# Two transformer blocks on one core: transposes of values a unit later, moving weights at another start, sums for three norms in other places

## The chip, the cores and the metric

One core of a Trainium2 chip runs the program. The metric is the device time of one execution in microseconds (us), as the median of several plain runs. The profiled execution is a further one, whose time is given beside its span.

## The reference, cut to what matters

Two blocks run one after the other on 256 tokens of width 1024, in fp32. In the first block 16 meta tokens are set ahead of the sequence, so that its products have 272 columns where keys and values need the meta tokens. It has a SwiGLU part, a mixer with two kinds of attention, and a second SwiGLU part. The second block has a mixer of convolution and retention, a cross attention to 256 memory tokens, and a squared-ReLU part.

```python
def first_block(x, ...):
    h = concat(pad, meta_tokens, x)
    h = h + 0.5 * swiglu(rms_norm(h, ffn1_norm), ffn1_w_in, ffn1_w_out)
    h = h + token_mixer(rms_norm(h, mix_norm), ...)   # qa ka va fa | qb kb vb | ga gb
    h = h + 0.5 * swiglu(rms_norm(h, ffn2_norm), ffn2_w_in, ffn2_w_out)
    return h[:, BLOCK:]

def token_mixer(h, ...):
    qa, ka, va, fa, qb, kb, vb, ga, gb = split(h @ w_in)
    # qa, ka, qb, kb: rms norm over each head of 64
    log_f = log_sigmoid(fa + forget_bias)             # its running sum enters the scores of fox
    y = sigmoid(ga) * (fox(qa, ka, va, log_f) @ w_branch_fox) \
      + sigmoid(gb) * (swa(qb, kb, vb, sinks, bias) @ w_branch_swa)
    return y @ w_out

def second_block(x, mem, ...):
    mem_n = rmsnorm(mem, norm_mem_w)
    h = x + head_group_mixer(rmsnorm(x, norm_mix_w), ...)   # cg/cu gated conv, rq rk rv rg retention
    h = h + cross(rmsnorm(h, norm_xattn_w) @ xq_w, mem_n @ xkv_w) @ xo_w
    h = h + square(relu(rmsnorm(h, norm_mlp_w) @ up_w)) @ down_w
    return rmsnorm(h, norm_f_w)
```

## The kernel before

All weights stay in HBM and are streamed once through SBUF, in chunks of 2048 columns of fp32, by SP's DMA queue (`raw`). Each piece of up to 1024 columns is split into two parts that TensorE takes in its fp32r form: ScalarE copies it to the upper part `hi` (line 321), VectorE subtracts that from `raw` and gets the lower part `lo` (line 337). Activations are kept as an upper and a lower part too (`XH`, `XL`; `AHf`, `ALf`; `MH`, `ML` for the memory). Each product is three matmuls, `XH·hi`, `XL·hi` and `XH·lo` (`mm3`, lines 512 to 514). There the weights are the stationary operand, 128 x 128, and the activations move, 256 or 272 columns.

Only `products_t` (lines 1016 to 1028) is the other way round: a tile of activations is stationary and 512 columns of weights move. It makes the retention's values (`rv`, one call) and the memory's values (`xv`, two calls), with 8 `k` times 2 halves times 3 matmuls in each call, 144 in all.

`_part` (line 308) places the parts of a chunk in a tile that is 64 columns wider than the chunk, from a column that `shift` gives: `SHIFT` = 13 columns (52 bytes), or `SHIFT1` = 16 columns (64 bytes) for chunks that begin with a weight of `WITH_META`.

The order is written by hand. The program is a row of units, each made by `_Core.step` (line 401): the unit's matmuls `mm`, then a `hook`, then the evacuations of the unit before (`pending`), then background work `back`, then splits of weights ahead. Evacuations are generators: a plain `yield` lets one piece of weights be split, and `yield LATER` puts the rest off to the next unit's turn. So an evacuation's first part is issued after the next unit's matmuls, and what stands behind a `yield LATER` a unit after that. On each engine instructions run in this issued order.

PSUM has eight banks, five named `ps` and three `po`; `bank()` (line 449) hands them out in turn.

The places that the change touches:

- `value` (line 870): factors a value by the row factor `r` into `x` (line 872) and `rep` on VectorE, then has TensorE transpose both into a bank (lines 878 to 880), and a unit later copies it out: `vfm` (line 889) on VectorE, the rest on ScalarE. It serves the four units `va` and the unit `vb`. The projections run `ka`, `qa`, `fa`, `va`, `kb`, `qb`, `vb` and gates, and the attention's pairs of scores (line 669) begin between the unit `qb` 0 and the next.
- `key_s` and `key_like` (line 812): the sliding window's key, with squares (`sqh`), their sum per head by a matmul (line 778), a root, and the write to `ks`.
- `forget` (lines 790 to 810): a running sum over the tokens on VectorE, whose last step are two DMAs from POOL's queue (lines 809, 810) into rows of `kz`, which the scores read.
- `memory` (line 1002): background work during the second SwiGLU part, `f2` and `d2`: loads the memory, splits it into `MH` and `ML`, and adds its squares up in `accm`.
- `mixer2` (line 1031): the hook `stats` after the first unit of the convolution, `glu((0, 1))`, makes the row factor `r` of the mixer (line 561 and ScalarE's Ln and Exp, lines 555 and 556), and the memory's two factors `rm` and `rmc` (lines 1051 to 1055). The units' evacuations (`br`, `ar` line 1095, and so on) need `r`.

Of the kernel before, what the change touches and what calls it, by code (L numbers as in the profile page):

```python
# [10 lines left out]
F32 = mybir.dt.float32  # L11
# [15 lines left out]
SHIFT, SHIFT1 = 13, 16  # L27
WITH_META = ("f1g", "d1", "ka", "fa", "va")
DFF = 2816
MF = DFF // P  # L30
# [245 lines left out]
class _Weights:  # L276
# [3 lines left out]
    def __init__(self, nc, pool, ws):  # L280
        self.nc, self.pool, self.ws = nc, pool, ws
        chunks, self.where, self.start, self.ends, self.total = _plan()
        self.shift = [SHIFT1 if blocks[0][0][0] in WITH_META else SHIFT for blocks in chunks]
        self.raw, self.hi, self.lo = {}, {}, {}
        self.loaded = 0
        self.c, self.o = 0, 0
        self.begun = []
        self.done = 0
        self.used = 0
        self.free = 0  # L290
        self.beside = None
# [76 lines left out]
class _Core:  # L368
# [32 lines left out]
    def step(self, key, mm, evac=(), hook=None, bg=1, last=False, to=None,  # L401
             ahead=True, reach=1024):


        W = self.W
        end, to = W.span(key, to or key)
        W.split(end)
        mm()
        if hook:
            W.split(to)  # L410
            hook()
        work, self.pending = self.pending, []
        near = (min(to, W.done + reach) if last else to) if ahead else None
        self.run(work, near)
        self.pending = list(evac) + self.pending
        if last:
            W.split(near)
            self.drain()
        self.back(bg, to)
        if ahead:  # L420
            W.split(to)
# [8 lines left out]
def _program(ctx, tc, I, out, probe=None):  # L430
# [126 lines left out]

    def rms(acc, n):

        ps = bank()  # L560
        T.matmul(ps[:, :n], k0("ones"), acc, start=True, stop=True)
        r = tmp(base, "r")
        rsqrt(r[:, :n], ps[:, :n])
        return r
# [171 lines left out]
    def mixer(acc_in, acc_out):  # L736
        with tc.tile_pool(name="mixer", bufs=1, reuse_waits="tile") as pool:
# [73 lines left out]

            def key_like(ps, write):
                x = tmp(pool, "x", bufs=4)[:, :T1]
                V.tensor_tensor(x, ps[:, :T1], r[0][:, :T1], op=ALU.mult)
                yield
                root = head_norm(head_squares(x, T1), T1)
                yield LATER
                rc = root()
                yield
                for e in range(2):  # L820
                    write(e, slice(64 * e, 64 * e + 64), x, rc)
# [32 lines left out]
            def key_s(m, ps):  # L854
# [4 lines left out]

                return key_like(ps, write)  # L860

# [6 lines left out]
            def value(ps, dst, meta):  # L868
# [6 lines left out]
                                ps[:, SEQ:T1].unsqueeze(1).broadcast_to((P, H, NMETA)),  # L875
                                r[0][:, SEQ:T1].unsqueeze(1).broadcast_to((P, H, NMETA)), op=ALU.mult)
                vt = bank()
                T.transpose(vt[:, 0:P], x[:, :P], kc("id"))
# [122 lines left out]

    def memory(pool, MH, ML, accm):
        raw = pool.tile([P, KD, SEQ], F32, name="memraw")

        def one(k):
# [4 lines left out]
            add()  # L1010

        background.append(lambda: nc.sync.dma_start(raw, I["mt"]))
        background.extend([lambda: None] * 3)
        background.extend([lambda k=k: one(k) for k in range(KD)])

    def products_t(tag, j, x, evac, **kw):
# [14 lines left out]

    def mixer2(acc_in, acc_out, MH, ML, accm, kx, vx, rm, held):
        with tc.tile_pool(name="mixer2", bufs=1, reuse_waits="tile") as pool:
# [7 lines left out]
            cs = pool.tile([P, 2, SEQ], F32, name="cs")  # L1041
            rmc = pool.tile([P, 2], F32, name="rmc")
            nc.gpsimd.memset(U[:, :, :30], 0.0)
# [4 lines left out]
            def stats():  # L1048
                r.append(rms(acc_in[:, :SEQ], SEQ))
                ps, pc = bank(), bank()  # L1050
                T.matmul(ps[:, :SEQ], k0("ones"), accm, start=True, stop=True)
                for i in range(2):
                    T.matmul(pc[:, 2 * i : 2 * i + 2], accm[:, i * P : (i + 1) * P], k0("ones")[:, :2], start=True, stop=True)
                rsqrt(rm, ps[:, :SEQ])
                rsqrt(rmc, pc[:, 0:4:2])

# [20 lines left out]
            def glu(ms):  # L1077
                ab = {m: (bank(), bank()) for m in ms}

                def mm():  # L1080
                    cut = KD - 1 if len(ms) > 1 else KD
                    for part in (range(cut), range(cut, KD)):
                        for m in ms:
                            for k in part:
                                for o, t in zip(ab[m], "ug"):
                                    mm3(o[:, :SEQ], W.get(("c" + t, m, k)), xs(k), k == 0, k == KD - 1)

                def evac(m):
# [13 lines left out]
                step(("cg", ms[0], 0), mm, [lambda m=m: evac(m) for m in ms], hook=stats if ms[0] == 0 else None, bg=0,  # L1102
                     to=("cg", ms[-1], 0))

# [488 lines left out]
    accm = base.tile([P, SEQ], F32, name="accm")  # L1593
    rm = base.tile([P, SEQ], F32, name="rm")
    with tc.tile_pool(name="mem", bufs=1, side="right", reuse_waits="tile") as mpool:
        memory(mpool, MH, ML, accm)
        ffn("f2", "d2", SEQ, hB, "g_mix2", acc, acc2, bg=1, together=True)
# [5 lines left out]
    with tc.tile_pool(name="kvm", bufs=1, side="right", reuse_waits="tile") as kv:  # L1603
        kx = kv.tile([P, KD, SEQ], F32, name="kx")
        vx = kv.tile([P, 2, D], F32, name="vx")
        held = []
        mixer2(acc, acc2, MH, ML, accm, kx, vx, rm, held)
        probe("h4", hB)
# [21 lines left out]
```

## Time and profile before

| what | value |
|---|---|
| median of 3 plain runs | 954.95 us (954.78 to 955.3) |
| profiled execution | 955.88 us |
| its span in the trace | 954.1 us |
| mean granted clock of TensorE | 0.998 |
| busy: TensorE, VectorE, ScalarE, POOL | 99%, 71%, 56%, 1% of the span |
| read from HBM | 166.85 MB, 176 GB/s over the span |

The span runs from the first to the last recorded instruction; the execution's own time is 1.78 us longer. A matmul of 256 fp32r columns is recorded with some 280 ns although the next starts 113 to 120 ns later, because matmuls overlap in the array. For what one costs, the distance from one start to the next is read, not the duration. An idle time in brackets at the end of a row stands before that instruction, with the instruction that it waited for.

### The profile page before, as it was taken

To read this page: it belongs to the slowest core of one execution; us is meant where nothing else is said; L and a number is where in the kernel's file an instruction comes from. 1 tells how busy PE (TensorE), PEld (TensorE's weight loads), DVE (VectorE), ACT (ScalarE), POOL (GpSimd) and SP (SyncE) were. 2 spreads that over 40 slices of the span, in tenths; PEclk is the share of its full clock that TensorE was granted. 3 is DMA by queue.
4 is the path that set the end of the run, shared out by engine and by line. 5 is a ranking of instruction groups with operands and counts; after the bars stand their busy time and mean duration, and the time that the engine had idled before them with its cause. 6 is when DMAs were issued, how large, how long until landed. Compare 5 with 4: busy or idle time off the path is not lost.

```text
span 954.1 us, 18439 instructions
## 1 busy us (share of the span) xinstructions
PE 941.5 (99%) x7687; PEld 914.0 (96%) x7687; DVE 673.2 (71%) x1252; ACT 535.3 (56%) x930; POOL 10.2 (1%) x16
## 2 busy tenths in 40 slices
PE   9999999999999999999999999999999999999996
PEld 8999999999899999999999999888899999999996
DVE  6686556657886678678666667999976677775552
ACT  7555435446586566666544557546484566655441
POOL 0000000020000000000000000000000000000000
PEclk9999999999999999999999999999999999999999
DMA  9665527554333345655545565433543246655431
GB/s 327 197 253 177 177 91 243 175 181 176 133 133 130 107 144 193 238 198 208 180 176 179 196 244 212 162 133 140 217 164 143 89 177 221 211 196 212 177 133 45
DMA packets 30116, 169.12 MB, mean 177 GB/s; under 512 B 5048, under 2 KB 7488, under 8 KB 13392
## 3 DMA queue, kind: packets, MB, share of 16 engines
q1 hardware_dynamic: 29680, 167.41, 49.8%
q8 instruction: 60, 0.98, 0.4%
q10 hardware_dynamic: 288, 0.52, 0.1%
q14 instruction: 24, 0.20, 0.1%
q0 software_dynamic: 64, 0.01, 0.0%
HBM read 166.85 MB, written 1.07 MB: 176 GB/s over the span
## 4 chain that ended last, share of the span: by engine, by line
PE 71%; DVE 2%; ACT 2%; issue 0%; DVEq 0%; ACTq 0%
PE ps L512 14%; PE ps L513 14%; PE ps L514 14%; PE po L513 7%; PE po L512 7%; PE po L514 7%; PE ps L1028 1%; PE ps L1026 1%; PE ps L1027 1%; PE ps L669 1%; PE po L713 0%; DVE lo L337 0%; PE ps L1195 0%; DVE y L801 0%; PE po L1367 0%; PE ps L1329 0%
## 5 line engine op out<-in xcount | busy, mean ns | idle before, releaser
L337 DVE TENSOR_TENSOR lo<-raw,hi 128x1024 fp32r<-128x1024 f32 (+2 forms) x337 | 373.7, 1123 | 47.1 <-ACT hi L321 45.3
L321 ACT ACTIVATE hi<-raw 128x1024 fp32r<-128x1024 f32 (+2 forms) x337 | 322.0, 974 | 125.9 <-issue 44.1
L512 PE MATMUL ps<-XH,hi 128*128 128x256 f32 (+2 forms) x968 | 275.9, 285 | 0.5 <-ACT hi L321 0.5
L514 PE MATMUL ps<-XH,lo 128*128 128x256 f32 (+2 forms) x968 | 271.1, 280 | 0.0
L513 PE MATMUL ps<-XL,hi 128*128 128x256 f32 (+2 forms) x968 | 271.0, 280 | 0.0
L512 PEld LDWEIGHTS ps<-XH,hi 128*128 128x128 f32 (+1 forms) x968 | 181.1, 187 | 3.7 <-issue 1.3
L513 PEld LDWEIGHTS ps<-XL,hi 128*128 128x128 f32 (+1 forms) x968 | 181.5, 188 | 0.8
L514 PEld LDWEIGHTS ps<-XH,lo 128*128 128x128 f32 (+1 forms) x968 | 181.2, 187 | 0.5 <-DVE lo L337 0.2
L512 PE MATMUL po<-XH,hi 128*128 128x256 f32 (+1 forms) x464 | 131.6, 284 | 0.6 <-DVE ar L1095 0.6
L514 PE MATMUL po<-XH,lo 128*128 128x256 f32 (+1 forms) x464 | 130.1, 280 | 0.0
L513 PE MATMUL po<-XL,hi 128*128 128x256 f32 (+1 forms) x464 | 129.9, 280 | 0.0
L512 PEld LDWEIGHTS po<-XH,hi 128*128 128x128 f32 x464 | 87.4, 188 | 1.0 <-DVE ar L1095 0.8
L513 PEld LDWEIGHTS po<-XL,hi 128*128 128x128 f32 x464 | 87.2, 188 | 0.2
L514 PEld LDWEIGHTS po<-XH,lo 128*128 128x128 f32 x464 | 87.2, 188 | 0.0
L628 ACT ACTIVATE s<-gr 128x272 f32<-128x272 f32 (+1 forms) x44 | 18.7, 426 | 104.2 <-DVE gr L626 104.2
L512 PE MATMUL ps<-AHf,hi 128*128 128x272 f32 (+1 forms) x220 | 61.9, 281 | 0.0
L513 PE MATMUL ps<-ALf,hi 128*128 128x272 f32 (+1 forms) x220 | 61.9, 281 | 0.0
L514 PE MATMUL ps<-AHf,lo 128*128 128x272 f32 (+1 forms) x220 | 61.9, 281 | 0.0
L1066 DVE SCALAR_TENSOR_TENSOR cv<-U,par,cv 128x256 f32<-128x256 f32 x120 | 50.0, 475 | 0.2 <-ACT cv L1099 0.2
L514 PE MATMUL ps<-AHm,lo 128*128 128x256 f32 x160 | 44.2, 276 | 0.0
L512 PE MATMUL ps<-AHm,hi 128*128 128x256 f32 x160 | 44.2, 276 | 0.0
L513 PE MATMUL ps<-ALm,hi 128*128 128x256 f32 x160 | 44.2, 276 | 0.0
(391 smaller groups left out, 1780.2 us busy)
## 6 DMA issues: line engine op xcount, KB each, us to landing
raw<-in_ws_dram SPq DMA_DIRECT2D x128, 1024.0 KB, 4.9
raw<-in_ws_dram SPq DMA_DIRECT2D x32, 704.0 KB, 4.1
raw<-in_ws_dram SPq DMA_DIRECT2D x5, 512.0 KB, 6.7
dec<-in_dec_dram SPq DMA_DIRECT2D x1, 1536.0 KB, 7.4
hA<-in_xt_dram SPq DMA_DIRECT2D x2, 576.0 KB, 6.9
BM<-drow SPq DMA_DIRECT2D x2, 512.0 KB, 5.3
memraw<-in_mt_dram SPq DMA_DIRECT2D x1, 1024.0 KB, 7.0
cst<-in_cst_dram SPq DMA_DIRECT2D x1, 720.0 KB, 8.3
```

Source lines behind the costliest of these rows:

```text
L321: self.nc.scalar.activation(self.hi[c][:, a:b], self.raw[c][:, a:b], AF.Copy)
L337: self.nc.vector.tensor_tensor(self.lo[c][:, a:b], self.raw[c][:, a:b], self.hi[c][:, a:b].bitcast(F32), op=ALU.subtract)
L512: T.matmul(o, w[0], x[0], start=start, stop=False)
L513: T.matmul(o, w[0], x[1], start=False, stop=False)
L514: T.matmul(o, w[1], x[0], start=False, stop=stop)
L628: S.activation(s, gr, AF.Silu)
L669: T.matmul(ps[h][:, at : at + n], lhs, rhs, start=True, stop=True)
L1026: T.matmul(ps[i], xh[:, t], wh, start=k == 0, stop=False)
L1027: T.matmul(ps[i], xl[:, t], wh, start=False, stop=False)
L1028: T.matmul(ps[i], xh[:, t], wl, start=False, stop=k == KD - 1)
L1066: V.scalar_tensor_tensor(cv[:, m], U[:, m, j : j + SEQ], prm("cw", m * 31 + j), cv[:, m], op0=ALU.mult, op1=ALU.add)
```

## The change

Four things are changed; no instruction of the computation is added or left out.

1. `value` has a `yield LATER` ahead of its transposes, so that they are issued a unit later. `key_s` asks `key_like` for the same ahead of the sum per head (`late=True`).
2. Chunks that begin with `rv` or `xv` start at 16 columns (64 bytes) in place of 13 (52 bytes).
3. The sums and roots for `rm` and `rmc` go from `stats` into `memory`'s background work, after eleven empty turns, which is in the down projection `d2`; `rmc` becomes a tile of the base pool.
4. The sum for `r` is issued inside the first unit of the convolution, ahead of the products of its last `k` (12 matmuls), by the new function `mean`. The hook makes `r` from it before the last piece of 1024 columns is split (`keep`).

```diff
 WITH_META = ("f1g", "d1", "ka", "fa", "va")
+MOVING = ("rv", "xv")
 DFF = 2816
...
         chunks, self.where, self.start, self.ends, self.total = _plan()
-        self.shift = [SHIFT1 if blocks[0][0][0] in WITH_META else SHIFT for blocks in chunks]
+        self.shift = [SHIFT1 if blocks[0][0][0] in WITH_META + MOVING else SHIFT for blocks in chunks]
         self.raw, self.hi, self.lo = {}, {}, {}
...
     def step(self, key, mm, evac=(), hook=None, bg=1, last=False, to=None,
-             ahead=True, reach=1024):
+             ahead=True, reach=1024, keep=0):
...
         if hook:
-            W.split(to)
+            W.split(to - keep)
             hook()
...
-    def rms(acc, n):
+    def mean(acc, n):
...
         T.matmul(ps[:, :n], k0("ones"), acc, start=True, stop=True)
+        return ps
+    def rms(acc, n, ps=None):
+        ps = ps or mean(acc, n)
         r = tmp(base, "r")
...
-            def key_like(ps, write):
+            def key_like(ps, write, late=False):
                 x = tmp(pool, "x", bufs=4)[:, :T1]
...
                 yield
-                root = head_norm(head_squares(x, T1), T1)
+                sq = head_squares(x, T1)
+                if late:
+                    yield LATER
+                root = head_norm(sq, T1)
                 yield LATER
...
-                return key_like(ps, write)
+                return key_like(ps, write, late=True)
...
                                 r[0][:, SEQ:T1].unsqueeze(1).broadcast_to((P, H, NMETA)), op=ALU.mult)
+                yield LATER
                 vt = bank()
...
-    def memory(pool, MH, ML, accm):
+    def memory(pool, MH, ML, accm, rm, rmc):
         raw = pool.tile([P, KD, SEQ], F32, name="memraw")
...
+        def factors():
+            ps, pc = bank(), bank()
+            T.matmul(ps[:, :SEQ], k0("ones"), accm, start=True, stop=True)
+            for i in range(2):
+                T.matmul(pc[:, 2 * i : 2 * i + 2], accm[:, i * P : (i + 1) * P], k0("ones")[:, :2], start=True, stop=True)
+            yield LATER
+            rsqrt(rm, ps[:, :SEQ])
+            rsqrt(rmc, pc[:, 0:4:2])
         background.append(lambda: nc.sync.dma_start(raw, I["mt"]))
...
         background.extend([lambda k=k: one(k) for k in range(KD)])
+        background.extend([lambda: None] * 11)
+        background.append(factors)
...
-    def mixer2(acc_in, acc_out, MH, ML, accm, kx, vx, rm, held):
+    def mixer2(acc_in, acc_out, MH, ML, kx, vx, rm, rmc, held):
         with tc.tile_pool(name="mixer2", bufs=1, reuse_waits="tile") as pool:
...
             cs = pool.tile([P, 2, SEQ], F32, name="cs")
-            rmc = pool.tile([P, 2], F32, name="rmc")
             nc.gpsimd.memset(U[:, :, :30], 0.0)
...
             def stats():
-                r.append(rms(acc_in[:, :SEQ], SEQ))
-                ps, pc = bank(), bank()
-                T.matmul(ps[:, :SEQ], k0("ones"), accm, start=True, stop=True)
-                for i in range(2):
-                    T.matmul(pc[:, 2 * i : 2 * i + 2], accm[:, i * P : (i + 1) * P], k0("ones")[:, :2], start=True, stop=True)
-                rsqrt(rm, ps[:, :SEQ])
-                rsqrt(rmc, pc[:, 0:4:2])
+                r[0] = rms(acc_in[:, :SEQ], SEQ, r[0])
...
                                     mm3(o[:, :SEQ], W.get(("c" + t, m, k)), xs(k), k == 0, k == KD - 1)
+                        if ms[0] == 0 and cut in part:
+                            continue
+                        if ms[0] == 0:
+                            r.append(mean(acc_in[:, :SEQ], SEQ))
...
                 step(("cg", ms[0], 0), mm, [lambda m=m: evac(m) for m in ms], hook=stats if ms[0] == 0 else None, bg=0,
-                     to=("cg", ms[-1], 0))
+                     to=("cg", ms[-1], 0), keep=1024 if ms[0] == 0 else 0)
...
     rm = base.tile([P, SEQ], F32, name="rm")
+    rmc = base.tile([P, 2], F32, name="rmc")
     with tc.tile_pool(name="mem", bufs=1, side="right", reuse_waits="tile") as mpool:
-        memory(mpool, MH, ML, accm)
+        memory(mpool, MH, ML, accm, rm, rmc)
         ffn("f2", "d2", SEQ, hB, "g_mix2", acc, acc2, bg=1, together=True)
...
         held = []
-        mixer2(acc, acc2, MH, ML, accm, kx, vx, rm, held)
+        mixer2(acc, acc2, MH, ML, kx, vx, rm, rmc, held)
         probe("h4", hB)
...
```

The first place is TensorE's order between the units `va` 1 and `va` 2. `po_2852` is the bank of `va` 1's product, `x_2877` and `rep_2879` are `va` 0's factored value. Before:

```order
L513 MATMUL po_2852<-XL,hi_2724 128x272
L514 MATMUL po_2852<-XH,lo_2725 128x272
L878 MATMUL po_2881<-cst,x_2877 128x128
L879 MATMUL po_2881<-cst,x_2877 128x128
L880 MATMUL po_2881<-cst,rep_2879 128x128
L512 MATMUL po_2900<-XH,hi_2724 128x272
L513 MATMUL po_2900<-XL,hi_2724 128x272
```

After:

```order
L515 MATMUL po_2852<-XH,lo_2725 128x272
L513 MATMUL po_2852<-XH,hi_2724 128x272
L514 MATMUL po_2852<-XL,hi_2724 128x272
L515 MATMUL po_2852<-XH,lo_2725 128x272
L513 MATMUL po_2896<-XH,hi_2724 128x272
```

The three transposes of `va` 0 no longer stand between the two units; they come after the products of `va` 2.

The second place is TensorE's order ahead of the first pair of scores. `sqh` are the squares of the sliding window's key, `kz` and `qz` the keys and queries of the first pair. Before:

```order
L513 MATMUL po_3027<-XL,hi_2892 128x256
L514 MATMUL po_3027<-XH,lo_2893 128x256
L778 MATMUL po_3062<-sqh_3060,cst 128x272
L669 MATMUL ps_3068<-kz,qz 128x144
L669 MATMUL ps_3069<-kz,qz 128x144
```

After:

```order
L514 MATMUL ps_3021<-XL,hi_2888 128x256
L515 MATMUL ps_3021<-XH,lo_2889 128x256
L888 MATMUL po_3056<-cst,x_3009 128x128
L889 MATMUL po_3056<-cst,x_3009 128x128
L890 MATMUL po_3056<-cst,rep_3011 128x128
L675 MATMUL ps_3064<-kz,qz 128x144
```

The key's sum has gone from there (it comes after the products of the next unit, `qb` 1) and the transposes of `va` 3 have come.

The third place is TensorE's order at the end of the convolution's first unit. `acc` and `accm` hold the sums of squares of the rows and of the memory, and `po_7168` and `po_7169` are banks of the next unit. Before:

```order
L512 MATMUL ps_7041<-XH,hi_7000 128x256
L513 MATMUL ps_7041<-XL,hi_7000 128x256
L514 MATMUL ps_7041<-XH,lo_7001 128x256
L561 MATMUL ps_7154<-acc_4778,c_72 128x256
L1051 MATMUL ps_7159<-accm,c_72 128x256
L1053 MATMUL po_7160<-c_72,accm 128x2 x2
L512 MATMUL po_7168<-XH,hi_7044 128x256
L513 MATMUL po_7168<-XL,hi_7044 128x256
```

After, from the sum for `r` on:

```order
L514 MATMUL ps_7050<-XL,hi_7011 128x256
L515 MATMUL ps_7050<-XH,lo_7012 128x256
L562 MATMUL po_7143<-acc_4778,c_72 128x256
L513 MATMUL ps_7047<-XH,hi_6928 128x256
L514 MATMUL ps_7047<-XL,hi_6928 128x256
```

and in the down projection `d2`, where `AHf` are its activations:

```order
L514 MATMUL ps_6469<-ALf_4792,hi_6455 128x256
L515 MATMUL ps_6469<-AHf_4791,lo_6456 128x256
L1025 MATMUL ps_6546<-accm,c_72 128x256
L1027 MATMUL ps_6547<-c_72,accm 128x2 x2
L513 MATMUL ps_6565<-AHf_4791,hi_6463 128x256
```

One sum stands inside the unit, and the other two stand between two units of the down projection.

## Rows read from the trace of the kernel before

**Rows 1.** The page, part 1: engine, busy us (share of the span), instructions.
```profile
PE 941.5 (99%) x7687; PEld 914.0 (96%) x7687; DVE 673.2 (71%) x1252; ACT 535.3 (56%) x930; POOL 10.2 (1%) x16
```

**Rows 2.** PE's timeline: start, us, engine line, operation, tiles, shapes; [idle <-releaser].
```profile
241.37 0.29 PE L514 MATMUL po<-XH,lo 128*128 128x272 f32 x1
242.34 0.33 PE L878 MATMUL po<-cst,x 128*128 128x128 f32 x1 [0.68 <-DVE x L872]
...
246.59 0.30 PE L878 MATMUL ps<-cst,x 128*128 128x128 f32 x1 [0.74 <-DVE x L872]
...
249.79 0.29 PE L514 MATMUL ps<-XH,lo 128*128 128x272 f32 x1
249.93 0.27 PE L878 MATMUL ps<-cst,x 128*128 128x128 f32 x1
...
253.70 0.33 PE L878 MATMUL ps<-cst,x 128*128 128x128 f32 x1 [0.31 <-DVE x L872]
...
256.85 0.39 PE L778 MATMUL po<-sqh,cst 128*128 128x272 f32 x1
257.30 1.57 PE L669 MATMUL ps<-kz,qz 128*128 128x144 f32 x8
```

**Rows 3.** DVE's timeline, one row, and busy times by window (columns PE, PEld, DVE, ACT, POOL).
```profile
246.56 0.28 DVE L889 TENSOR_TENSOR vfm<-po,cst 128x128 f32<-128x128 f32 x1
...
246.00:254.00 8.00, 7.10 (x58) 6.91 (x58) 7.77 (x22) 3.37 (x5) 1.14 (x2) 1.00 0.39 132
```

**Rows 4.** POOL's timeline, and line 810's DMA from issue to landing.
```profile
253.10 0.52 POOL L810 DMA_DIRECT2D kz<-p  x1
...
DMA to landing us min/median/max: 2.6/2.6/2.6
```

**Rows 5.** PE's timeline in a unit of the memory's values, first and last.
```profile
659.82 0.40 PE L1026 MATMUL ps<-hi,MH 128*128 128x512 f32 x1
...
663.80 0.40 PE L1028 MATMUL ps<-lo,MH 128*128 128x512 f32 x1
```

**Rows 6.** PE's timeline, end of the convolution's first unit.
```profile
575.01 0.28 PE L512 MATMUL po<-XH,hi 128*128 128x256 f32 x1
...
576.26 0.28 PE L514 MATMUL ps<-XH,lo 128*128 128x256 f32 x1
576.37 0.59 PE L561 MATMUL ps<-acc,c 128*128 128x256 f32 x2
576.80 0.59 PE L1051 MATMUL ps<-accm,c 128*128 128x256 f32 x2
577.23 0.50 PE L1053 MATMUL po<-c,accm 128*128 128x2 f32 x4
...
577.92 0.28 PE L514 MATMUL po<-XH,lo 128*128 128x256 f32 x1
578.77 0.39 PE L512 MATMUL po<-XH,hi 128*128 128x256 f32 x1 [0.57 <-DVE ar L1095]
```

**Rows 7.** PE's timeline in a stretch of 256-column products, first and last.
```profile
709.81 0.28 PE L514 MATMUL po<-XH,lo 128*128 128x256 f32 x1
...
711.97 0.28 PE L514 MATMUL po<-XH,lo 128*128 128x256 f32 x1
```

**Rows 8.** Line 512's busy times by window (columns PE, PEld, clock, DMA, GB/s).
```profile
577.00:765.00 188.00, 97.14 (x337) 63.70 (x338) 1.00 0.42 151
```

**Rows 9.** Timelines of DVE and PE in the second block's mixer.
```profile
614.47 0.42 DVE L1112 TENSOR_TENSOR rx<-ps,cs 128x256 f32<-128x256 f32 x1 [0.56 <-PE ps L1109]
...
683.88 0.47 DVE L1066 SCALAR_TENSOR_TENSOR cv<-U,par,cv 128x256 f32<-128x256 f32 x1
...
685.02 0.81 PE L1290 MATMUL ps<-cv,cst 128*128 128x256 f32 x3
```

**Rows 10.** ACT's timeline, in the down projection and ahead of the convolution.
```profile
531.96 1.07 ACT L321 ACTIVATE hi<-raw 128x1024 fp32r<-128x1024 f32 x1 [1.52 <-issue]
...
567.44 1.28 ACT L425 ACT_TABLE_LOAD   x1
```

## Prediction

> **What bounds the kernel now.** I read the page first: TensorE (PE) is busy for 941.5 of 954.1 us and no other engine comes near [rows 1]. So an edit is worth what it takes off PE's own row of instructions: an idle stretch in front of an instruction, or the spacing of matmuls in an unbroken stream. Work taken off VectorE (DVE) or ScalarE (ACT) is worth nothing unless PE waits for it. I then listed PE's waits and went to the timeline at the four places that the diff touches, taking starts of successive instructions rather than durations, since PE's recorded ends overlap. In each timeline the reader should see the step from one start to the next: 0.11 to 0.14 us is a running stream, more is a hole.
>
> The time needed is a median of plain runs (954.95). The profiled execution took 955.88: its span of 954.1 and 1.78 outside it. It lies 0.93 above the median, so I make the sum on the span and take the difference off the median. About 0.2% (1.9 us) is what a measurement of this kernel can tell from no change; 0.2% below the median is 953.04, above it 956.86.
>
> **Part 1, values' transposes and the last key's sum.** The first transpose of a value waits for `x`, which DVE writes after the unit's matmuls: PE starts 0.97 us after the unit's last matmul (241.37 to 242.34, idle 0.68) [rows 2]. Where `x` was ready the step is 0.14 (249.79 to 249.93). The lost time is 0.97 − 0.14 = 0.83, which is the idle time plus 0.15. The other two waiting places have idles of 0.74 and 0.31, hence 0.89 and 0.46 [rows 2]. In sum **2.2 us**. The reason for the wait is DVE's queue: from 246 to 254 it is busy for 7.77 of 8.00 us [rows 3]. One unit later `x` is at least 3 us old, so these waits go whole. The instructions stay: three transposes per value, only later in PE's row. `vfm`, the evacuation of the transposes, moves a unit later with them (0.28 us of DVE each), and its readers come only with the attention, after the last unit.
>
> What is late next? The first attention scores (line 669, at 257.30 [rows 2]) read `kz`, whose last rows are written by the forget gate's two DMAs. The last is issued on POOL at 253.10 and lands 2.6 us later, at 255.7 [rows 4]. If PE comes 2.2 us earlier it is there before that. The DMA itself moves up little: its chain runs on DVE, which is full, and only one `vfm` (0.28 us or less [rows 3]) leaves the queue ahead of it; I take 255.5. The second product of the pair is the first that reads these rows. The four products of the row (144, 144, 272 and 272 columns) take 1.57, so one of 144 takes 0.27 and the second began about 257.57; at most 257.57 − 255.5 = 2.07 of the 2.2 can be kept up to here. Of this, 0.45 is not a gain but the key's sum (256.85 to 257.30 [rows 2]), which only moves behind the next projection unit, and is paid there: 1.62 net. After that the banks that the next scores write are released by softmax on DVE, whose queue has hardly moved; I leave 0.27 for that, an estimate of about one short DVE instruction (`vfm`'s 0.28). **Part 1: −1.35.** Bounds: −2.0, when the DMA lands earlier by as much as PE does; −0.4, when all of the forget chain, the softmax and the banks stay where they are in time and only one of the three holes is kept.
>
> The key's own path (root, `ks`) is later by one unit. `ks` is read first by the sliding-window scores, four pairs later: cost 0, hidden by four pairs of attention.
>
> **Part 2, moving weights at 64 bytes.** In `products_t` the weights are the moving operand, 512 columns wide. From 659.82 to 663.80 there are 18 rows in one stream, 17 steps: 3.98/17 = 234 ns each [rows 5]. It runs in 48 matmuls for `rv` and 96 for `xv`, 144 in all. What can a start of 52 or of 64 bytes change? The trace has one clue: streams of 256-column matmuls run at two rates. From 575.01 to 576.26 there are 12 rows in 11 steps, 113.6 ns [rows 6]; from 709.81 to 711.97 19 rows in 18 steps, 120.0 ns [rows 7], both in a stretch whose granted clock is 1.00, the level of 2.4 GHz [rows 8]. The difference of 6.4 ns is 16 columns at 2.4 GHz (6.7 ns), that is 64 bytes of fp32. I read it as one more 64-byte line read for a row. A row of 2048 bytes that starts at byte 52 touches 33 such lines, at byte 64 32. So my estimate is 6.4 ns a matmul: 144 × 6.4 = **−0.9 us**. This is the weakest term. Its lower end is zero: that the two rates have another cause and a start changes nothing. A loss I exclude, as 64 bytes cover the fewest possible lines whatever the line. The upper end is set by what is late next on DVE: in the stretch of `rv`, `rx` waits 0.56 for PE, after which DVE is the later one; in the stretch of `xv` the last tap of the convolution starts 683.88, lasts 0.47 with no idle before it, and PE reads `cv` at 685.02, so PE can come 0.67 earlier at most [rows 9]. So 0.56 + 0.6 = −1.16 at the most.
>
> The Trainium skill ("SBUF — State Buffer", the note on cachelines) speaks of lines of 16 bytes. By these, byte 52 makes 129 lines of 128: 1.7 ns a matmul, an estimate of 0.24 us in place of 0.9. The row of 6.4 ns fits 64 bytes better. The same skill ("TensorE: Matmul & The Clock Gate", "Back-to-back issue gap") gives N/2.4 + 2.5 ns for a matmul by itself, 216 at 512 columns, where 234 is measured; that would leave 144 × 18 = 2.6 us to gain before the bounds above. At 256 columns it gives 109 and the best stream here shows 113.6, so I don't count on it.
>
> **Parts 3 and 4, memory's factors and the row factor.** At the end of the convolution's first unit PE does three things in a row: the sum for `r` (576.37 to 576.80, 0.43), the one for memory's `rm` (576.80 to 577.23, 0.43) and four tiny rows for `rmc` (from 577.23, 0.50) [rows 6]. All of it is still done, elsewhere. So moving it gains nothing by itself. The hole behind it is the gain: the second half of the next unit starts 0.85 us after the row before it (577.92 to 578.77), with 0.57 of waiting on `ar`, the DVE evacuation of the unit before [rows 6]. It waits for a bank: four accumulators of the first unit, three banks for the sums, two of the next unit are nine of eight. Afterwards the sums for `rm` and `rmc` are gone from there, and seven are enough. Besides, `r` is made earlier: its sum comes 12 matmuls before the unit's end, which is 12 × 0.1136 = 1.36 us, so ACT's two instructions and with them the evacuations come about that much earlier too. 0.85 less the 0.11 of a running step is 0.74; the restart after the fp32 rows takes about 0.1 more, which goes with it: **−0.85**. Bounds: −1.0 and −0.4 (half of it comes back as a later wait for the same evacuation).
>
> Where `rm` and `rmc` go, in the down projection of the feed-forward part, PE pays the same 0.43 and some 0.4 us. ACT has to load another function table there (1.28 us, as it does now at 567.44) and do four short activations, the ones that it did behind the convolution's first unit; that stage has idle ACT time in every unit, 1.52 us before the row at 531.96 for one [rows 10], and the weights are split several us ahead of use. Cost 0, covered by that lead; without the cover it would be up to 1.3. The load at 567.44 goes in return. `acc` itself is complete before the convolution's first unit begins, so that its sum finds it ready. SP's and POOL's queues keep their order.
>
> **The sum.** −1.35 − 0.9 − 0.85 = −3.1. Span 954.1 → 951.0, profiled execution about 952.8, median 954.95 − 3.1 = **951.85**.
>
> **The rivals.**
> - *Alignment gives nothing* (part 2 = 0): −2.2, 952.75. For it: the two rates are seen on one stream's moving activations, whose start never changes, so a phase of PE could be the cause as well as a line. Chance 0.2. By the skill's 16-byte lines (above) it would be 0.24 less, an estimate.
> - *Part 1 is eaten*: PE meets the forget DMA, softmax and banks and keeps 0.4 only. −0.4 − 0.5 − 0.85 = −1.75, with part 2 between its two cases; 953.2, not to be told from no change. For it: DVE is full just there [rows 3] and keeps its own time. Against: there is a stretch of slack behind each unit in which it could catch up. Chance 0.17.
> - *All of it at its upper ends*: −2.0 − 1.16 − 0.85 = −4.0, 950.9. Chance 0.09. A matmul spacing by the skill's isolated gap (above) ends here too, since DVE's ends hold it.
> - *Slower*: streams of matmuls change over from 113.6 to 120.0 ns. Such phases begin and end at breaks in the stream, and the change moves the fp32 rows that make the breaks. Each changed matmul costs 6.4 ns; to end 1.9 above the median after a gain of 3.1, 5.0 us or 780 more matmuls must be at the slow rate. The stretch from 577 to 765 has 3 × 337 = 1011 of the kind [rows 8], so most of it would have to change: 957. Chance 0.04. A smaller shift of this sort, ±0.7, is in the range.
>
> **How the numbers follow.** Forecast 0.5, rivals 0.2, 0.17, 0.09, 0.04. The range goes from 950.3 (the upper ends with a lucky 0.6 of phases) to 954.2 (part 1 eaten, part 2 nothing: −1.25, and 0.5 of unlucky phases). Faster by over 0.2% needs −1.9: all of the forecast but a small part (0.45), most of the second case (0.13), all of the fourth (0.09), 0.03 of the third: 0.70. Slower 0.04. Within 0.2%: 0.26.
>
> **What would show it.** Right: no idle before the value's transposes, and scores(0) with a wait of up to 0.8 for POOL's DMA; 512-column steps of 227 to 228 ns in place of 234; no wait for `ar` in the second conv unit, and no new wait in the down projection around the memory sums. Wrong: steps of 234 still; a wait before the `ks` or `vfm` readers; `lo` becoming a releaser in the down projection; 120-ns stretches where there were 113.6, or the other way, over more than a few hundred matmuls.

## The result and the profile after

The changed kernel takes 976.37 us (median; 976.04 to 976.57) beside 955.12 for the kernel before on the same chip: a ratio of 1.0219, 95% interval 1.0207 to 1.0231. The forecast was 951.9, in a range of 950.3 to 954.2. It went the other way, by seven times what was forecast.

The first thing to read is what did *not* happen. These are PE's waits in the changed kernel, in the list of what each line waited for (us in total, times, longest):

```profile
PE ps L576 <- POOL cosr L1576: 1.1, 1, 1.1
PE ps L1482 <- ACT sq L1469: 1.0, 1, 1.0
PE po L1375 <- DVE p L1368: 0.2, 1, 0.2
PE ps L675 <- DMA kz<-p: 0.2, 1, 0.2
```

The waits of the values' transposes for `x` [rows 2] and of the second conv unit for `ar` [rows 6] are gone, as forecast, and no new one of any size has come. PE waits less than before, and the program is 20 us longer. So it is not a wait: PE is busy longer. The page says the same:

```profile
span 974.4 us, 18437 instructions
PE 964.4 (99%) x7687; PEld 937.5 (96%) x7687; DVE 674.8 (69%) x1252; ACT 535.0 (55%) x930; POOL 10.2 (1%) x16
```

The same 7687 matmuls take 964.4 us in place of 941.5 [rows 1], at the same granted clock. What one matmul costs is read from the starts. This is PE's timeline in the first block's second SwiGLU, first of before, then of after; the rows left out are matmuls of the same kind:

```profile
399.66 0.28 PE L514 MATMUL po<-XH,lo 128*128 128x256 f32 x1
...
402.04 0.28 PE L514 MATMUL ps<-XH,lo 128*128 128x256 f32 x1
```

```profile
399.74 0.28 PE L515 MATMUL po<-XH,lo 128*128 128x256 f32 x1
...
402.14 0.28 PE L514 MATMUL ps<-XL,hi 128*128 128x256 f32 x1
```

In before there are 22 rows, 21 steps in 2.38 us: 113.3 ns. In after 21 rows, 20 steps in 2.40 us: 120.0 ns. It is no passing phase. The windows below count line 512's matmuls (513's in after), one in three of a stream, in stretches of the first block's SwiGLU parts and of the last one (columns: PE busy with count, PEld, granted clock, DMA share, GB/s). Before, then after:

```profile
100.00:200.00 100.00, 77.45 (x271) 50.91 (x271) 1.00 0.53 179
400.00:480.00 80.00, 64.91 (x236) 44.21 (x236) 1.00 0.55 197
880.00:940.00 60.00, 48.71 (x177) 33.15 (x177) 1.00 0.38 134
```

```profile
100.00:200.00 100.00, 77.21 (x271) 50.88 (x271) 1.00 0.52 179
400.00:480.00 80.00, 62.70 (x223) 41.74 (x222) 1.00 0.49 181
880.00:940.00 60.00, 47.70 (x171) 31.96 (x170) 1.00 0.54 193
```

The granted clock is 1.00 (2.4 GHz) in all of them. The first stretch, 272 columns, is as fast as it was. From 200 us on, streams of 256 columns do fewer matmuls in the same time. I added up, over all steps of such streams (those within 20 ns of it), what each takes beyond 113.3 ns (256 columns) or 123.3 ns (272): 4.2 us in the kernel before, **27.2 us** in the changed one. The difference of 23.0 is the loss and the 2 to 3 us that the edits gained beside it. In the experiments on addresses below, the same sum is 29.9 (spacer), 29.8 (64 bytes), 35.6 and 35.1 (the two with other shifts), 3.2 and 15.0 (256 and 128 bytes), and 34.9 and 16.9 (weights, activations moved).

### The profile page after: what moved, and what is told of

Same layout as the page of the kernel before. It is cut to its first block, busy times and chain, and to the rows that moved or that the text cites. A ratio compares the mean times of both kernels' runs of the same rounds, so it can differ in the third digit from the quotient of the medians.

```text
span 974.4 us, 18437 instructions
## 1 busy us (share of the span) xinstructions
PE 964.4 (99%) x7687; PEld 937.5 (96%) x7687; DVE 674.8 (69%) x1252; ACT 535.0 (55%) x930; POOL 10.2 (1%) x16
## 4 chain that ended last, share of the span: by engine, by line
PE 72%; DVE 2%; ACT 1%; issue 0%; DMA 0%; DVEq 0%; POOL 0%; ACTq 0%
PE ps L513 14%; PE ps L515 14%; PE ps L514 14%; PE po L515 7%; PE po L514 7%; PE po L513 7%; PE ps L1048 1%; PE ps L1050 1%; PE ps L1049 1%; PE ps L675 1%; PE po L719 0%; PE ps L1214 0%; PE po L1386 0%; DVE lo L338 0%; PE ps L1348 0%; PE po L734 0%
## 5 line engine op out<-in xcount | busy, mean ns | idle before, releaser
L513 PE MATMUL ps<-XH,hi 128*128 128x256 f32 (+2 forms) x984 | 283.8, 288 | 0.0
L514 PE MATMUL ps<-XL,hi 128*128 128x256 f32 (+2 forms) x984 | 278.6, 283 | 0.0
L515 PE MATMUL ps<-XH,lo 128*128 128x256 f32 (+2 forms) x984 | 278.4, 283 | 0.0
L513 PE MATMUL po<-XH,hi 128*128 128x256 f32 (+1 forms) x448 | 128.2, 286 | 0.0
L515 PE MATMUL po<-XH,lo 128*128 128x256 f32 (+1 forms) x448 | 126.9, 283 | 0.0
L514 PE MATMUL po<-XL,hi 128*128 128x256 f32 (+1 forms) x448 | 126.8, 283 | 0.0
L513 PEld LDWEIGHTS po<-XH,hi 128*128 128x128 f32 x448 | 84.2, 188 | 0.2
L513 PE MATMUL ps<-AHf,hi 128*128 128x272 f32 (+1 forms) x198 | 56.2, 284 | 0.0
L515 PE MATMUL ps<-AHf,lo 128*128 128x272 f32 (+1 forms) x198 | 56.2, 284 | 0.0
L514 PE MATMUL ps<-ALf,hi 128*128 128x272 f32 (+1 forms) x198 | 56.1, 283 | 0.0
```

Of the source, the lines that this page charges most:

```text
L513: T.matmul(o, w[0], x[0], start=start, stop=False)
L514: T.matmul(o, w[0], x[1], start=False, stop=False)
L515: T.matmul(o, w[1], x[0], start=False, stop=stop)
```

## Two explanations

*Order.* The forecast had a rival of this kind, at 0.04: the fp32 rows between the streams have moved, and streams change over to 120 ns at such breaks. But the loss is in stages that the change doesn't touch, such as the second SwiGLU and the last part.

*Addresses.* The change makes `rmc` a tile of the base pool, of 2 columns. A tile takes at least 32 bytes, and what is allocated later lies 32 bytes further on: the weights' parts `hi` and `lo`, and the activations of each stage (`AHf`, `OFH`, `CH`, `OXH`, `AHm`). `XH`, `XL` and `MH` are allocated earlier and stay. All other tiles of the base pool have widths that are multiples of 64 columns, 256 bytes. The list of changes names the move of `rmc`, and the prediction gives it no term. Where a tile starts follows from the sizes of the tiles ahead of it in the code, so the starts below are worked out, and the times are measured. That the move is 32 bytes is borne out by the last run of experiment 3 below: with 32 bytes taken off the weights' shift, `XH`'s streams are back at 113.3 ns.

## Experiments: is it the addresses

**1. Addresses without the order, and the order without them.** The kernel before with a spacer:

```diff
     rm = base.tile([P, SEQ], F32, name="rm")
+    spacer = base.tile([P, 2], F32, name="spacer")
+    nc.gpsimd.memset(spacer, 0.0)
```

> The kernel before, in its own order, with an unused tile of 2 columns (32 bytes, cleared once by POOL) behind `rm` in the base pool: nothing but the addresses behind it moves. Theory A (addresses): slower by some 20 to 24 us, 975 to 979, with 256-column streams at 120 ns. Theory B (order): 955, as before.

Measured: 980.86, ratio 1.0262 (1.0238 to 1.0285). Addresses alone, in the kernel before with its own order, cost 25.7 us. So the loss doesn't need the new order.

The changed kernel with `rmc` in 16 columns (this pads it to 64 bytes; later runs to 128 and 256):

```diff
-    rmc = base.tile([P, 2], F32, name="rmc")
+    rmc = base.tile([P, 16], F32, name="rmc")[:, :2]
```

> The changed kernel with one difference: the tile of `rmc` in the base pool is 16 columns wide (64 bytes) in place of 2 (padded to 32), so that every tile behind it (the weights' parts, the activations of each stage) starts at the same byte of a 64-byte line as in the kernel before. Theory A, the 32 bytes of the new base tile made the loss: the streams run at 113.3 ns again, and the four edits give what they give: 951 to 953.5 us. Theory B, the new order of the fp32 rows made the streams change over to 120 ns: no change against the changed kernel, 975 to 977.

Measured: 979.12, ratio 1.0244 (1.0225 to 1.0264). This theory failed in its number: bytes in a line of 64 are not what counts.

Two more runs were laid out on the same idea of 64 bytes, and with the failed idea they don't part the weights' start from the activations':

> The changed kernel with its 2-column `rmc`, but SHIFT and SHIFT1 at 21 and 24, so that the weights' parts start at byte 52 and byte 0 of a 64-byte line as intended, while the activations of the stages (AHf, CH, OXH, AHm) stay moved by 32 bytes. Theory A1, the weights' start alone decides: 951 to 954. Theory A2, the activations' start alone decides: some 976. Both in part: between, about 962. Theory B (order): 976.

> The changed kernel with `rmc` padded to 64 bytes, so that the activations start where they did, but SHIFT and SHIFT1 at 5 and 8, so that the weights' parts start at bytes 20 and 32 of a line, as they do in the changed kernel. Theory A1, the weights' start alone decides: some 975. Theory A2, the activations' start alone: 951 to 954. Theory B (order): 976, but then e1_pad is 976 too.

Measured: 984.25 (ratio 1.0298, 1.0278 to 1.0317) and 983.88 (1.0294, 1.0275 to 1.0314). Both are slower than the changed kernel. None of the answers laid out for them was right; they became useful afterwards as points of the table below.

**2. The step.** `rmc` in 64 and in 32 columns (256 and 128 bytes), the rest as changed:

> The changed kernel with `rmc` in a tile of 64 columns (256 bytes), as wide as the step to which all other tiles of the base pool are rounded. The 64 bytes of e1_pad did not bring the time back, yet e2_before_spacer showed that moved addresses alone make the loss, so the step that counts would be longer than 64 bytes. Theory A (addresses, in steps of 128 or 256 bytes): 113.3-ns streams return and the time is that of the forecast's sum, 951 to 953.5. Theory C (any move of these tiles hurts, or something else that a further tile brings): 976 to 984.

> The same with 32 columns (128 bytes). If the step is 128 bytes: as e5_pad256, 951 to 953.5. If it is 256: slow in streams as the others, 965 to 984.

Measured: 952.96 with 256 bytes, ratio 0.9978 (0.997 to 0.9986); 964.57 with 128 bytes, ratio 1.0098 (1.0081 to 1.0115). The step is not 128 bytes. With 256 bytes the loss is gone and the four edits show their gain; the sum over the steps is 3.2 us, from 27.2. The windows of line 513 in that kernel have the counts of before:

```profile
100.00:200.00 100.00, 77.45 (x271) 50.86 (x270) 1.00 0.53 178
400.00:480.00 80.00, 64.96 (x236) 44.15 (x236) 1.00 0.57 198
880.00:940.00 60.00, 48.69 (x177) 33.13 (x177) 1.00 0.34 124
```

So 23 us hang on how wide a tile of two useful columns is made, with the order of the changed kernel kept. This version is also the fastest of the three: 2.1 us below the kernel before, which takes 955.07 beside it.

**3. Whose start.** With the step of 256 bytes known, the weights and the stages' activations are moved one at a time. The weights alone, by 32 bytes, in the 256-byte version:

```diff
-SHIFT, SHIFT1 = 13, 16
+SHIFT, SHIFT1 = 21, 24
```

> e5_pad256 with SHIFT and SHIFT1 at 21 and 24: the weights' parts start 32 bytes further on, the activations where they were. Theory R, a stream's rate goes by the distance of the weights' start from the activations' start: all 256-column streams run at 120 ns, as in e3_w_back, where the distance was the same in the stages' own tiles; 980 to 985. Theory W, only streams of the activations that lie in the base pool (XH, MH) feel the weights' start, and the other tiles feel their own: 968 to 974, with AHf, CH, OXH and AHm at 113.3.

The stages' activations alone, by 32 bytes (the changed kernel, whose weights are put back to the bytes of before):

```diff
-SHIFT, SHIFT1 = 13, 16
+SHIFT, SHIFT1 = 5, 8
```

> The changed kernel with its 2-column `rmc`, and SHIFT and SHIFT1 at 5 and 8, so that the weights' parts start at the very bytes of the kernel before, while the stages' tiles of activations (AHf, OFH, CH, OXH, AHm) stay moved by 32 bytes. XH did not move, so by either theory its streams run at 113.3 again. Theory R (distance, here 20 bytes as in e4_w20): AHf and AHm at 120, the 272-column AHf at 125.3; about 965. Theory X (the activations' own start: as in the changed kernel): AHm at 117.8, AHf at 113.5 to 120; 957 to 961. If the activations' start has no part: 953.

Measured: 983.65 (ratio 1.0295, 1.0276 to 1.0314) and 966.26 (1.0113, 1.0095 to 1.0132), both near the times that theory R, the distance between the two, put them at. The rates that it named came in part: in the second run `AHm` is at 120.0 as foretold, but the 256-column `AHf` at 117.9 in place of 120 and the 272-column one at 126.6 in place of 125.3. Line 513's windows, of the weights moved first, then of the activations moved:

```profile
100.00:200.00 100.00, 77.00 (x271) 50.78 (x271) 1.00 0.54 179
400.00:480.00 80.00, 62.54 (x222) 41.56 (x222) 1.00 0.52 178
880.00:940.00 60.00, 46.99 (x168) 31.40 (x167) 1.00 0.55 193
```

```profile
100.00:200.00 100.00, 76.93 (x267) 50.00 (x266) 1.00 0.52 173
400.00:480.00 80.00, 64.95 (x236) 44.10 (x235) 1.00 0.54 190
880.00:940.00 60.00, 47.20 (x167) 31.38 (x168) 1.00 0.44 157
```

In the second, the stretch at 400 (`XH`, whose distance is that of before) has its 236 again, while the stretch at 880 (`AHm`) has 167 of 177, though the weights lie where they lay. Neither start decides alone: each of them, moved by itself, makes streams slow. Put together over the runs, by the distance from the activations' tile to the weights' start, in bytes modulo 256 (mean spacing in ns; ranges where runs differ):

| stream | fast | slow |
|---|---|---|
| 256 columns, `XH` (400 to 500 us) | 52: 113.3 | 84: 120.0; 116: 119.0; 180: 118.2 |
| 256 columns, `OFH`, `OS`, `OXH` | 52, both tiles moved together by 0 to 256 bytes: 113.3 to 114.4 | 20: 116.7 to 120.6; 84: 120.0 to 120.1 |
| 272 columns, `XH` (0 to 100 us) | 64 or 96: 123.3 to 123.5 | 128: 126.6 to 126.7; 192: 126.7 |
| 272 columns, `AHf` (100 to 200 us) | 64 or 96: 123.3 to 123.4 | 32: 125.3 and 126.6 |
| weights moving, 512 columns | 64: 228.8 to 228.9 | 52, 84, 96, 192: 233.2 to 233.5; 128: 232.5 to 233.3 |

(`OS` is the output of the sliding-window attention. Steps at a stream's start are in the means.) For `XH` the distance and the weights' own start move together, since `XH` stays; it is the second row, where both tiles move and the rate stays, that speaks for the distance.

The distance does not say all. `AHm` has a distance of 52 in four placements: 113.3 to 113.4 where its own tile lies as before or 128 bytes further, 117.8 with both tiles 32 bytes further, 120.0 with both 64 further. And at one placement `AHf` ran at 120 and then, after the rows of memory's factors had broken the stream, at 113.5 (538.53 in the changed kernel), or at 120 throughout (in the kernel with the spacer, which has no such rows there). That last difference explains about 2 us of the 4.5 by which the spacer's kernel is slower than the changed one, the rest is about the edits' gain. So where tiles start changes a stream's rate, and it isn't all that does. That a break can choose between two rates is what these two kernels suggest, and the 64-byte version, which changes over at the same rows; they differ in more than that break, and no run moves the break alone. What in the memory or the engine makes it so isn't shown by any run.

## Experiments: what the four edits are worth

All of these compare with the 256-byte version (952.96; its runs lie between 952.5 and 954.2). Differences of 0.5 to 0.9 us are near what a median of 8 to 12 runs can tell, so each is read in the trace too. Together the three come to 2.2, beside the 2.1 by which the 256-byte version is faster than the kernel before.

**4. Part 2 taken out** (the 256-byte version, weights of `rv` and `xv` back at byte 52):

```diff
-MOVING = ("rv", "xv")
+MOVING = ()
```

> e5_pad256 with the moving weights of rv and xv back at byte 52 (MOVING empty). The forecast's reading (one 64-byte line less, 6.4 ns for each of 144 matmuls): 0.9 us more than e5_pad256. The rival, that alignment gives nothing here, for which speak the 233.3 ns at starts of 96, 0 and 32 bytes seen so far: the same within 0.2 us.

Measured: 953.45, ratio to before 0.9981 (0.9972 to 0.9989), so 0.5 us for part 2. The rows of the memory's values in the 256-byte version:

```profile
658.35 0.39 PE L1048 MATMUL ps<-hi,MH 128*128 128x512 f32 x1
...
663.38 0.39 PE L1049 MATMUL ps<-hi,ML 128*128 128x512 f32 x1
```

23 rows, 22 steps: 228.6 ns beside 234 [rows 5]; over all 144 matmuls 228.9 against 233.4. That is 4.5 ns, 0.65 us in all. The 0.5 in the time agrees with it, but the runs of the two versions overlap (952.5 to 954.2 and 952.9 to 954.3), so by itself it shows no gain; the spacing does.

**5. Part 1 taken out:**

```diff
-                return key_like(ps, write, late=True)
+                return key_like(ps, write)
...
-                yield LATER
                 vt = bank()
```

> e5_pad256 without part 1: the values' transposes and the last key's sum stand where they did. The forecast: 1.35 us more than e5_pad256 (0.4 to 2.0). The rival that the forget gate's DMA and softmax eat part 1: 0 to 0.4 more.

Measured: 953.76, ratio to before 0.9986 (0.9977 to 0.9994): 0.8 us for part 1. PE's timeline at the first scores, of the 256-byte version and then of the one without part 1:

```profile
254.79 0.41 PE L675 MATMUL ps<-kz,qz 128*128 128x144 f32 x2
256.24 1.40 PE L675 MATMUL ps<-kz,qz 128*128 128x144 f32 x6 [1.03 <-DMA kz<-p]
```

```profile
257.53 1.57 PE L675 MATMUL ps<-kz,qz 128*128 128x144 f32 x8
```

The first scores come 2.74 us earlier. Then the second product stands until the forget gate's DMA has landed. It was issued at 253.19 (POOL's timeline of the 256-byte version) and landed 2.9 us later (line 816's DMA there, from issue to landing):

```profile
252.57 0.64 POOL L815 DMA_DIRECT2D kz<-p  x1 [39.93 <-DVE p L814]
253.19 0.52 POOL L816 DMA_DIRECT2D kz<-p  x1
```

```profile
DMA to landing us min/median/max: 2.9/2.9/2.9
```

At the last of the fox scores, where the key's sum has been paid for and the banks have had their say, PE is 0.74 us ahead (starts 284.44 and 285.18), and 0.73 at the start of the fox output's projection (341.38 and 342.11).

**6. The last key's sum back in its place**, since PE stands there anyway:

```diff
-                return key_like(ps, write, late=True)
+                return key_like(ps, write)
```

> e5_pad256 with the last key's sum back ahead of the first scores (late=True taken away), the values' transposes still a unit later. In e5_pad256 the second scores product waits 1.0 us for the forget gate's DMA. If that DMA alone sets the time there, the key's sum (0.45 us) is free in front of it, and 0.3 to 0.45 us are gained: 952.5 to 952.7. If the softmax and its banks set the time behind it, nothing is gained: 952.9 to 953.1.

Measured: 952.96, ratio 0.9975 (0.9965 to 0.9985): no difference. The time is that of the second answer, but for neither of the reasons given. PE does not stand for the DMA any more, but it stands 1.5 us for the sum's own squares, which ACT has not made by then:

```profile
255.85 0.73 PE L784 MATMUL po<-sqh,cst 128*128 128x272 f32 x2 [1.51 <-ACT sqh L777]
```

With the holes closed, PE is too early for the key's squares, and `late=True` takes it past them to meet the DMA instead. One wait is exchanged for another, and `late=True` is worth nothing that the time shows: the gain of part 1 comes with the later transposes alone.

**7. Parts 3 and 4 taken out** (the kernel before with parts 1 and 2, no new base tile):

> The kernel before with parts 1 and 2 alone: no new base tile, memory's factors and the row factor where they were. The forecast: 0.85 us more than e5_pad256, 953.8, by the hole of 0.74 that stays ahead of the second half of the convolution's second unit. If the hole would have gone elsewhere: as e5_pad256, 953.0.

Measured: 953.85, ratio 0.9986 (0.9977 to 0.9995): 0.9 us for parts 3 and 4 (0.8 by the ratios to the kernel before). The hole stands again in that kernel, in its timeline:

```profile
575.47 0.59 PE L562 MATMUL ps<-acc,c 128*128 128x256 f32 x2
575.90 0.59 PE L1056 MATMUL ps<-accm,c 128*128 128x256 f32 x2
576.33 0.50 PE L1058 MATMUL po<-c,accm 128*128 128x2 f32 x4
...
577.86 0.39 PE L513 MATMUL po<-XH,hi 128*128 128x256 f32 x1 [0.57 <-DVE ar L1100]
```

In the 256-byte version the sum for `r` stands inside the unit and the stream goes on behind it without a wait:

```profile
575.28 0.28 PE L515 MATMUL ps<-XH,lo 128*128 128x256 f32 x1
575.40 0.59 PE L562 MATMUL po<-acc,c 128*128 128x256 f32 x2
575.64 0.47 PE L513 MATMUL ps<-XH,hi 128*128 128x256 f32 x1
575.94 0.28 PE L514 MATMUL ps<-XL,hi 128*128 128x256 f32 x1
```

## Why the prediction was wrong

**The step that failed** is the one at which nothing was written. The working of parts 3 and 4 says of `rm` and `rmc` where their sums go, and costs PE's and ACT's time there, but says nothing of the line that makes `rmc` a tile of the base pool, although that line was in the diff. It moved everything allocated behind it by 32 bytes, and that cost about 23.4 us (976.37 against 952.96, with the same order and the same instructions). With that line at 256 bytes the time is 952.96, inside the range and 1.1 above the forecast.

**The price was in the working itself, read from rows that don't show it.** Part 2 read the two rates of [rows 6] and [rows 7] as the same matmul with one 64-byte line more, and put a price of 6.4 ns on where a tile starts, for 144 matmuls. The same price on the program's other matmuls of 256 columns, more than 4000, would have been over 25 us: the question "which tiles does this change move?" was asked for two weights only. That where data lies can set the rate is right. The line of 64 bytes was wrong, since the 64-byte pad brought nothing back, and a start at byte 0 or 32 of such a line left the 512-column matmuls at 232 to 233 ns in the kernels whose weights had moved. And the two rows are not a case of it. This is the stretch of [rows 7] where its slow rate begins and ends, in the kernel before:

```profile
696.24 0.28 PE L514 MATMUL ps<-CH,lo 128*128 128x256 f32 x1
...
697.72 0.28 PE L512 MATMUL po<-CH,hi 128*128 128x256 f32 x1
698.06 0.39 PE L513 MATMUL po<-CL,hi 128*128 128x256 f32 x1
698.29 0.28 PE L514 MATMUL po<-CH,lo 128*128 128x256 f32 x1
...
699.73 0.28 PE L514 MATMUL po<-CH,lo 128*128 128x256 f32 x1
...
717.13 0.59 PE L561 MATMUL ps<-acc,c 128*128 128x256 f32 x2
```

Up to 697.72 there are 13 steps of 113.8 ns; behind one gap, from 698.29 on, 12 steps of 120.0, with the same `CH` and the same chunk of weights, and so it goes on up to the fp32 sum at 717.13. The 256-byte version stays at 113.3 ns behind the same gap. So the first rival's doubt, a phase of PE, fits [rows 7] better than an address does, and it is in part luck that the term of part 2 came near. (The phase has about 157 steps; at 6.7 ns more it costs an estimated 1.0 us, near the 0.93 by which the profiled execution lies above the median.)

**The slow rival** had the right symptom (streams at 120 ns, 5 us needed, priced at 957) and the wrong cause, the order of the fp32 rows, and so the wrong size: it looked for streams near the rows that move, 1011 matmuls from 577 to 765. An address has no place in the order, and it reached streams from 200 us to the end. The spacer's run, which keeps the order, decides against the cause named. Phases of the kind that the rival describes exist, as `AHf` shows, but there it is a matter of 2 us and not of 21.

**The four edits, by themselves:**
- *Part 1*, forecast −1.35 (−0.4 to −2.0), measured −0.8. The holes went whole, and the limit named was the right one: the forget DMA, with a wait of 1.03 where "up to 0.8" was foretold. The DMA landed at about 256.1 to 256.2, not 255.5: the last issue did not move up with the shorter DVE queue (253.19 beside 253.10 [rows 4], and 253.22 in the version without part 1), and its landing took 2.9 in place of 2.6. That is 0.6 us, as much as is missing. Moving the key's sum, the other half of part 1, gained nothing (experiment 6).
- *Part 2*, forecast −0.9, measured −0.5 in the time and −0.65 by the spacing. The mis-sized term is the 6.4 ns a matmul: 4.5 were measured. It was seen only at a distance of 64 bytes, which the 256-byte version has and the changed kernel has not: there the spacing is 233.3, so that part 2 gained nothing.
- *Parts 3 and 4*, forecast −0.85, measured −0.8 to −0.9. `ar`'s wait is gone and the down projection is longer by the moved rows alone (0.88 us, against 0.83 foretold), with no wait of PE there, so that the table load is hidden. Of the two reasons given, it is the bank count: in the 256-byte version PE starts the fourth matmul of the second unit while VectorE is still at work on `ar`, which an earlier `r` alone would not allow:

```profile
577.33 0.42 DVE L1114 SCALAR_TENSOR_TENSOR ar<-ps,r 128x256 f32<-128x256 f32 x1
```

```profile
577.54 0.28 PE L513 MATMUL po<-XH,hi 128*128 128x256 f32 x1
```

The Trainium skill ("SBUF — State Buffer", the note on cachelines) gives lines of 16 bytes. By lines of that size alone, a move of 32 bytes changes no start within a line, and I would have expected it to cost nothing. The runs show that this is not enough: 32 bytes cost 25.7 us in the kernel before.

## What to carry to other kernels

A new tile in a long-lived pool moves every tile behind it. Before costing an edit in instructions, list which tiles change their start, and give a small tile the full step of its neighbours (here 256 bytes), or put it where nothing lies behind it. If a change makes all streams slower with no new waits, compare the spacing of matmuls in a stage that the change doesn't touch: when that has moved, look at addresses, and test it by the kernel before with an unused tile of the same size.

## What the runs showed of the hardware that was not expected

- The same fp32r matmul of 256 columns, in an unbroken stream at the same granted clock, takes 113.3 to 120.0 ns a step by where the stationary and the moving operand start. Of the widths tried for the new tile, only 256 bytes kept the rates (32, 64 and 128 bytes gave 976, 979 and 965 us; 256 gave 953).
- Both starts count (weights alone moved by 32 bytes: 983.65; activations alone: 966.26). `OFH`, `OS` and `OXH` keep 113.3 to 114.4 ns while the distance stays, so that the distance is much of it, but `AHm` went from 113.3 to 117.8 and 120.0 at a constant distance.
- At the same placement a stream can run at either rate, and the rate was seen to change at breaks: `AHf` at 120 ns ahead of memory's sums and 113.5 after, `CH` in the kernel before at 113.8 and then 120.0 behind a gap of one matmul.
